# The down projection as seven block products instead of eight, in sixteen passes that add into SBUF

## The chip, the cores and the metric

One core of a Trainium2 chip runs the whole kernel as one program. The metric is the device time of one execution in microseconds. A profiled execution has, beside its time, a span: the stretch from the first to the last recorded instruction.

## What is computed

The reference is one encoder block on 512 tokens of width 2048, all in float32. The attention half is the same in both kernels. The change is in the second matrix product of the feed-forward half:

```
u = rmsnorm(x, norm_mlp_g) @ w_up            # 512 x 8192
x = x + square(relu(u)) @ w_down             # 8192 x 2048, the down projection
return rmsnorm(x, norm_final_g)
```

TensorE multiplies in a reduced format. So each float32 operand is split into a rounded high part and the rest (`wh` and `wl` of a weight, two halves of one tile for an activation), and three matmuls (high·high, high·low, low·high) stand for one. The split costs a cast on ACT and a subtraction on DVE per operand tile.

## The kernel before, in words

The stages run one after the other: attention, output projection, up projection, down projection, final norm.

The **up projection** (lines 579 to 612) makes u transposed, 32 blocks q of 256 features. Each block is a 2x2 block product with seven products instead of eight: `quad` (line 460) loads four weight blocks `b` from HBM and makes four sums of them on DVE (line 469), `parts` splits the seven weight operands (lines 94 and 95), and `prod` (line 583) runs 24 matmuls of 128x256 for each. The relu and square follow at line 611, and POOL stores 512 KB of the result to the DRAM tensor `ud` (line 612).

The **down projection** (lines 615 to 690) is a plain product. The 8192 features are cut into four chunks g of 2048. For each chunk, eight loads `ur` (line 629) bring the activations from `ud`, and each is split into `uT` (line 630). Then come four passes n over 512 output columns each. In a pass eight weight units u are loaded and split (`load_unit`, lines 72 to 91, the pools `raw`, `wh` and `wl` with three buffers each), and each serves all four token tiles t: `mm3` (lines 97 to 100) issues three matmuls of 128x512 for each of its two k tiles. After a pass four DVE instructions add the four PSUM banks, times the per-token factor `qs`, to the residual `x1` in SBUF (`add`, line 644).

There are 16 such passes of 192 matmuls, 3072 in all. The last pass (lines 659 to 690) goes token tile by token tile instead: each tile's sum of squares, `rstd_of` (line 102), four scalings and four output DMAs follow while TensorE works on the next tile. Only the fourth tile's chain is left behind the last matmul.

The code is written through a scheduler: `tc.high_priority(offset=...)` lets an instruction take an earlier place on its engine, but each engine and each queue then runs its list in the listed order. SP issues nearly all loads, POOL the stores to DRAM. The pool `rx` has six buffers of 512 KB, shared by the blocks `b` of the up projection and the `ur` tiles.

## Time and profile before

| quantity | value |
|---|---|
| median of 3 runs | 2201.66 us (2200.47 to 2202.65) |
| profiled execution, its own time | 2200.84 us |
| its span | 2199.1 us |
| TensorE busy (matmuls) | 2169.4 us, 99% of the span |
| VectorE (DVE) busy | 1241.8 us, 56% |
| ScalarE (ACT) busy | 834.8 us, 38% |
| GpSimd (POOL) busy | 211.3 us, 10% |
| DMA engines, mean rate | 125 GB/s |

The profiled execution's time is 1.74 us longer than its span; this part lies around the recorded instructions. An engine's share says how long it had something in work. It doesn't say that the end waits for it: that is read from the chain of work that ended last, and from the idle time in front of an engine's instructions. DMA-issuing instructions are not counted as busy time of their engine.

### The profile page before, as it was taken

The numbers are of one execution on the slowest core, as the hardware profiler recorded it, in microseconds if no ns is written. First come the engines' busy times: TensorE is split into PE (matmuls) and PEld (weight loads), VectorE is DVE, ScalarE is ACT, GpSimd is POOL, SyncE is SP. The second block draws the span as 40 slices with busy tenths as digits, with TensorE's granted clock in tenths as the row PEclk, the third lists the DMA queues.
The fourth block names the chain that finished last, engine by engine and source line by source line (L and its number), as shares of the span: only waits on it lengthen the run. The fifth ranks groups of instructions, "written<-read, shape, count | busy, mean of one in ns | idle before, by whom it ended". The sixth has DMA issues, their size and how long they took to land.

```text
span 2199.1 us, 31164 instructions
## 1 busy us (share of the span) xinstructions
PE 2169.4 (99%) x12988; PEld 1938.2 (88%) x12988; DVE 1241.8 (56%) x1462; ACT 834.8 (38%) x1191; POOL 211.3 (10%) x189
## 2 busy tenths in 40 slices
PE   7999999999999998999999999999999999999998
PEld 6889989888988888999999999998888888888886
DVE  6656566565574448777778777774233334234233
ACT  4444444444454434444444444442122123113232
POOL 5222122122120000000000000000000000000002
PEclk9999999999999999999999999999999999999999
DMA  6332232232243632333343334347234235223242
GB/s 214 116 110 86 92 110 88 90 110 91 78 145 135 222 110 97 125 132 128 125 145 130 127 127 144 135 147 275 98 120 156 96 100 169 96 96 115 98 142 87
DMA packets 79533, 275.26 MB, mean 125 GB/s; under 512 B 9696, under 2 KB 9888, under 8 KB 78880
## 3 DMA queue, kind: packets, MB, share of 16 engines
q1 hardware_dynamic: 69312, 240.29, 32.7%
q0 software_dynamic: 9648, 32.46, 4.5%
q8 instruction: 101, 1.65, 0.3%
q10 hardware_dynamic: 432, 0.53, 0.1%
q14 instruction: 40, 0.33, 0.0%
HBM read 240.73 MB, written 30.25 MB: 123 GB/s over the span
## 4 chain that ended last, share of the span: by engine, by line
PE 97%; DVE 1%; ACT 1%; issue 1%; DMA 0%; SPq 0%; ACTq 0%; DVEq 0%
PE pm L587 29%; PE pm L100 11%; PE pm L99 11%; PE pm L98 11%; PE pa L141 8%; PE pa L100 7%; PE pa L99 7%; PE pa L98 7%; PE pb L100 1%; PE pb L99 1%; PE pb L98 1%; PE pc L100 1%; PE pc L99 1%; PE pc L98 1%; PE pc L291 1%; PE pc L292 1%
## 5 line engine op out<-in xcount | busy, mean ns | idle before, releaser
L90 DVE TENSOR_TENSOR wl<-raw,wh 128x1024 fp32r<-128x1024 f32 (+1 forms) x219 | 269.3, 1230 | 518.3 <-ACT wh L89 517.2
L89 ACT CAST wh<-raw 128x1024 fp32r<-128x1024 f32 (+1 forms) x250 | 262.3, 1050 | 672.9 <-PE pm L100 470.6
L99 PE MATMUL pm<-wl,uT 128*128 128x512 f32 x968 | 376.6, 389 | 0.0
L100 PE MATMUL pm<-wh,uT 128*128 128x512 f32 x968 | 376.6, 389 | 0.0
L98 PE MATMUL pm<-wh,uT 128*128 128x512 f32 x968 | 376.6, 389 | 0.0
L587 PE MATMUL pm<-s,wh 128*128 128x256 f32 x1536 | 281.2, 284 | 3.8 <-ACT p L592 2.2
L587 PE MATMUL pm<-a,wh 128*128 128x256 f32 x1536 | 274.8, 282 | 0.8 <-ACT wh L94 0.8
L587 PEld LDWEIGHTS pm<-s,wh 128*128 128x128 f32 x1536 | 240.8, 193 | 4.5 <-ACT p L592 2.4
L587 PEld LDWEIGHTS pm<-a,wh 128*128 128x128 f32 x1536 | 235.5, 189 | 1.2 <-ACT wh L94 1.0
L95 DVE TENSOR_TENSOR wl<-ts,wh 128x1024 fp32r<-128x1024 f32 x128 | 154.9, 1223 | 117.5 <-ACT wh L94 117.5
L587 PE MATMUL pm<-s,wl 128*128 128x256 f32 x768 | 218.2, 284 | 0.0
L98 PEld LDWEIGHTS pm<-wh,uT 128*128 128x128 f32 x968 | 181.7, 188 | 37.8
L99 PEld LDWEIGHTS pm<-wl,uT 128*128 128x128 f32 x968 | 181.7, 188 | 37.8
L100 PEld LDWEIGHTS pm<-wh,uT 128*128 128x128 f32 x968 | 181.7, 188 | 37.7
L141 PE MATMUL pa<-wh,hT 128*128 128x256 f32 x1024 | 200.7, 290 | 13.7 <-DVE hT L166 7.3
L587 PE MATMUL pm<-a,wl 128*128 128x256 f32 x768 | 212.1, 282 | 0.0
L94 ACT CAST wh<-ts 128x1024 fp32r<-128x1024 f32 x128 | 132.7, 1052 | 196.1 <-PE pm L587 180.3
L100 PE MATMUL pa<-hT,wl 128*128 128x512 f32 x512 | 201.5, 394 | 0.0
L99 PE MATMUL pa<-hT,wh 128*128 128x512 f32 x512 | 200.9, 392 | 0.0
L98 PE MATMUL pa<-hT,wh 128*128 128x512 f32 x512 | 200.4, 391 | 0.0
L141 PEld LDWEIGHTS pa<-wh,hT 128*128 128x128 f32 x1024 | 167.9, 197 | 18.2 <-DVE hT L166 8.5
L94 ACT CAST wh<-b 128x1024 fp32r<-128x1024 f32 x96 | 101.0, 1052 | 160.4 <-PE pm L587 121.3
(240 smaller groups left out, 3432.7 us busy)
## 6 DMA issues: line engine op xcount, KB each, us to landing
b<-in_w_up SPq DMA_DIRECT2D x128, 512.0 KB, 3.7
raw<-in_w_down SPq DMA_DIRECT2D x128, 512.0 KB, 3.3
raw<-in_w_out SPq DMA_DIRECT2D x32, 512.0 KB, 3.6
ud<-c POOLq DMA_DIRECT2D x32, 512.0 KB, 3.1
ur<-ud SPq DMA_DIRECT2D x32, 512.0 KB, 4.8
raw<-in_w_dq SPq DMA_DIRECT2D x16, 512.0 KB, 3.3
raw<-in_w_dk SPq DMA_DIRECT2D x16, 512.0 KB, 3.3
raw<-in_w_nv SPq DMA_DIRECT2D x16, 512.0 KB, 3.4
```

The costliest lines, as they stand in the source:

```text
L89: nc.scalar.copy(out=wh[:, cs], in_=raw[:, cs])
L90: eng.tensor_sub(out=wl[:, cs], in0=raw[:, cs], in1=wh[:, cs].bitcast(F32))
L94: nc.scalar.copy(out=hi, in_=src)
L95: (eng or nc.vector).tensor_sub(out=lo, in0=src, in1=hi.bitcast(F32))
L98: nc.tensor.matmul(out=ps, lhsT=lh, rhs=rh, start=first, stop=False)
L99: nc.tensor.matmul(out=ps, lhsT=lh, rhs=rl, start=False, stop=False)
L100: nc.tensor.matmul(out=ps, lhsT=ll, rhs=rh, start=False, stop=last)
L141: nc.tensor.matmul(out=ps[t], lhsT=a, rhs=b[:, k, :], start=first and i == 0, stop=last and i == 2, skip_group_check=True)
L291: nc.tensor.matmul(out=ps, lhsT=xq[:, s, ts], rhs=kx[:, s, :], start=True, stop=False)
L292: nc.tensor.matmul(out=ps, lhsT=xq[:, s, ts], rhs=ky[:, s, :], start=False, stop=True)
L587: nc.tensor.matmul(out=ps, lhsT=a[:, k], rhs=b[:, k], start=first and k + i == 0, stop=last and k == 7 and i == 2, skip_group_check=True)
```

## The change

Now the down projection too is made of 2x2 block products. The features are cut into eight chunks c of 1024, the output columns into two halves n of 1024, which gives sixteen passes. The tokens are split in two halves of 256, the chunk's features in two halves of 512, and the column half into two blocks h of 512. A pass has seven products of 24 matmuls of 128x512: 168 instead of 192.

**Operands of a chunk** (`chunk_operands`): four `ur` loads in rows of 1 KB (after, line 628), four sums on DVE (lines 638, 641, 645, 647) and seven splits, in the same `rx` pool. **Weights of a pass** (`down_weights`): ten plain loads by SP (line 661), four more loads issued by POOL that add onto a block already loaded (line 663, `accum_op`), for the sums t1 = b11+b12 and t3 = b22+b12; two sums t2 and t4, two tiles each, on DVE (line 669); fourteen splits.

**Results** (`to_y`): no product is scaled; each is added to one or two of the four quarters of y in SBUF. Of the seven additions of a pass, five are DVE instructions on 128x2x512 with one operand in PSUM (line 753). The other two (first and sixth product) are an ACT copy (line 750) and a DMA by POOL that adds onto y (line 751). In chunk 0 the first write of each quarter is an ACT copy (line 747).

**The end**: x1 is no longer held in SBUF. In the last pass `finish` (lines 701 to 704) loads it in pieces, scales y by `qs` and adds it, and takes the squares; `times_g` (line 708) multiplies by the final gain; `norm_out` (lines 711 to 725) does the norm and the output DMAs of one token tile. The tiles 0 and 1 are finished first. The seventh product is cut in two blocks of 128 tokens, b = 0 and b = 1, and line 798 adds each to y.

The core of the diff:

```
+    psD = ctx.enter_context(tc.tile_pool(name="psD", bufs=4, space=bass.MemoryType.PSUM, reuse_waits="tile"))
+    wd = ctx.enter_context(tc.tile_pool(name="wd", bufs=11, reuse_waits="tile"))
+    y = ypool.tile([P, NT, DM], F32, name="y")
+    def chunk_operands(c):
+        def load(m, th):
+            t = rx.tile([P, 4, 256], F32, name="ur", tag="b")
+            nc.sync.dma_start(out=t, in_=ud[4 * c:4 * c + 4, :, (2 * m + th) * 256:(2 * m + th + 1) * 256].rearrange(
+                "j p t -> p j t"))
+            return t
+        with tc.high_priority(offset=700):
+            u11, u22, u21, u12 = load(0, 0), load(1, 1), load(0, 1), load(1, 0)
...
+            nc.vector.tensor_sub(out=f1, in0=u22, in1=u21)
+            split(o[0][:, 0], o[0][:, 1], u11)
+            split(o[1][:, 0], o[1][:, 1], f1)
+            nc.vector.tensor_add(out=f2, in0=f1, in1=u11)
...
+            nc.vector.tensor_sub(out=f2, in0=f2, in1=u12)
+            split(o[3][:, 0], o[3][:, 1], f2)
+            nc.vector.tensor_sub(out=u11, in0=u11, in1=u21)
...
+    def down_weights(c, n):
+        def load(u, i, j=None):
+            with tc.high_priority(offset=ah):
+                t = wd.tile([P, 1024], F32, name="b", tag="b")
+                nc.sync.dma_start(out=t, in_=w_down[c, n, u, i])
+                if j is not None:
+                    nc.gpsimd.dma_start(out=t, in_=w_down[c, n, u, j], accum_op=ALU.add)
+            return t
...
+        yield [parts(load(u, 0)) for u in range(2)]
+        t1 = [load(u, 0, 1) for u in range(2)]
+        yield [parts(t) for t in t1]
+        b22 = [load(u, 3) for u in range(2)]
+        t2 = [add(t1[u], b22[u]) for u in range(2)]
+        yield [parts(t) for t in t2]
...
-        for n in range(4):
-            cs = slice(n * 512, (n + 1) * 512)
-            po = [psm() for _ in range(NT)]
...
+            def to_y(ps, th, h, neg, fresh=False, dma=False):
+                ys = y[:, 2 * th:2 * th + 2, n * 1024 + h * 512:n * 1024 + h * 512 + 512]
+                if c == 0 and fresh:
+                    nc.scalar.mul(ys, ps, -1.0 if neg else 1.0)
+                elif dma:
+                    st = wd.tile([P, 2, 512], F32, name="st", tag="st", bufs=2)
+                    nc.scalar.copy(out=st, in_=ps)
+                    nc.gpsimd.dma_start(out=ys, in_=st, accum_op=ALU.add)
+                else:
+                    nc.vector.tensor_tensor(out=ys, in0=ys, in1=ps, op=ALU.subtract if neg else ALU.add)
...
+            w11, w1, w2 = next(ops), next(ops), next(ops)
+            prod(pU, o[0], w11, True)
+            to_y(pU, 0, 0, False, fresh=True, dma=not end)
+            prod(pW, o[1], w1, True)
+            to_y(pW, 1, 1, True, fresh=True)
...
+            for b in range(2):
+                prod(pU, o[6], w4, False, blocks=(b,))
+                ys = y[:, 2 + b, 1024:1536]
+                nc.vector.tensor_add(out=ys, in0=ys, in1=pU[:, b])
+                finish(2 + b, 1, 0, 1)
+                norm_out(2 + b, 2)
```

Three places where the lists of the engines change. First the border between up and down projection. The list of DVE before, from the next to last result of the last up block to the first weight units (`c` is a result of the up projection, `uT` an activation operand, `wl` a weight's low part):

```order
L605 SCALAR_TENSOR_TENSOR c<-pm,p_14512 128x256
L90 TENSOR_TENSOR wl<-raw,wh 128x1024
L95 TENSOR_TENSOR uT<-ur,uT 128x1024
L607 SCALAR_TENSOR_TENSOR c<-pm,u_14482 128x256
L95 TENSOR_TENSOR uT<-ur,uT 128x1024
L90 TENSOR_TENSOR wl<-raw,wh 128x1024
L95 TENSOR_TENSOR uT<-ur,uT 128x1024 x2
L611 SCALAR_TENSOR_TENSOR c<-c 128x1024
L90 TENSOR_TENSOR wl<-raw,wh 128x1024 x8
```

DVE now, from the same result (line 608) on. Some rows ahead of it stands the last but one result (line 606, 605 before), and right behind that the operand sum of line 647:

```order
L608 SCALAR_TENSOR_TENSOR c<-pm,u_14482 128x256
L95 TENSOR_TENSOR uT<-ur,uT 128x1024
L645 TENSOR_TENSOR uf<-uf,ur 128x1024
L95 TENSOR_TENSOR uT<-ur,uT 128x1024 x2
L612 SCALAR_TENSOR_TENSOR c<-c 128x1024
L95 TENSOR_TENSOR uT<-uf,uT 128x1024
L95 TENSOR_TENSOR wl<-b,wh 128x1024 x2
L638 TENSOR_TENSOR uf<-ur 128x1024
L641 TENSOR_TENSOR uf<-uf,ur 128x1024
L669 TENSOR_TENSOR ts<-b 128x1024
L95 TENSOR_TENSOR wl<-b,wh 128x1024
```

The two splits of the first product's weights stand at `wl<-b x2`. Behind them now come two sums for the operands of chunk 1 (lines 638 and 641), ahead of the sum and the split that the second product needs. SP's list before, at the border:

```order
L465 DMA b<-in_w_up 128x1024 x122
L629 DMA ur<-ud 128x1024 x4
L80 DMA raw<-in_w_down 128x1024
L629 DMA ur<-ud 128x1024
L80 DMA raw<-in_w_down 128x1024
L629 DMA ur<-ud 128x1024 x5
L80 DMA raw<-in_w_down 128x1024 x2
L629 DMA ur<-ud 128x1024 x2
L80 DMA raw<-in_w_down 128x1024
```

SP's list now:

```order
L465 DMA b<-in_w_up 128x1024 x122
L628 DMA ur<-ud 128x4x256 x6
L661 DMA b<-in_w_down 128x1024 x11
L628 DMA ur<-ud 128x4x256 x2
L661 DMA b<-in_w_down 128x1024 x15
```

The first six `ur` loads are the four of chunk 0 and two of chunk 1. They stand ahead of the first eleven weight loads, and the other two loads of chunk 1 behind them.

Second, the steady state on DVE. One pass before, between two passes' additions to the residual:

```order
L90 TENSOR_TENSOR wl<-raw,wh 128x1024 x8
L644 SCALAR_TENSOR_TENSOR x_0_14617<-pm,qs,x_0_14617 128x512
L644 SCALAR_TENSOR_TENSOR x_1_14618<-pm,qs,x_1_14618 128x512
L644 SCALAR_TENSOR_TENSOR x_2_14619<-pm,qs,x_2_14619 128x512
L644 SCALAR_TENSOR_TENSOR x_3_14620<-pm,qs,x_3_14620 128x512
L90 TENSOR_TENSOR wl<-raw,wh 128x1024 x8
```

Now, the second half of a pass with n = 1, in which the next chunk's operands are made:

```order
L95 TENSOR_TENSOR uT<-ur,uT 128x1024 x2
L95 TENSOR_TENSOR wl<-b,wh 128x1024
L753 TENSOR_TENSOR y<-y,pd 128x2x512
L95 TENSOR_TENSOR wl<-b,wh 128x1024
L638 TENSOR_TENSOR uf<-ur 128x1024
L95 TENSOR_TENSOR uT<-ur,uT 128x1024
L95 TENSOR_TENSOR wl<-b,wh 128x1024
L95 TENSOR_TENSOR wl<-ts,wh 128x1024
L641 TENSOR_TENSOR uf<-uf,ur 128x1024
L95 TENSOR_TENSOR wl<-ts,wh 128x1024
L669 TENSOR_TENSOR ts<-ts,b 128x1024
L753 TENSOR_TENSOR y<-y,pd 128x2x512
```

An addition (line 753) is no longer in a group at the pass's end but follows each product, with splits, sums and operands of later products between.

Third, the last pass. DVE before, the first token tile of four:

```order
L644 SCALAR_TENSOR_TENSOR x_0_14617<-pm,qs,x_0_14617 128x512
L679 TENSOR_TENSOR ssf<-v_18562,ssq 128x1
L105 TENSOR_SCALAR vf<-ssf 128x1
L107 RECIPROCAL rf<-rf 128x1
L108 TENSOR_TENSOR tf<-rf 128x1
L109 TENSOR_TENSOR tf<-tf,vf 128x1
L110 TENSOR_SCALAR tf<-tf 128x1
L111 TENSOR_TENSOR rf<-rf,tf 128x1
L684 SCALAR_TENSOR_TENSOR x_0_14617<-x_0_14617,rf,gF 128x512
L687 TENSOR_SCALAR x_0_14617<-x_0_14617,rf 128x512
```

DVE now, from behind the addition of the seventh product of the pass before and one split; the last split shown is the first one of the fourth product's weights:

```order
L702 SCALAR_TENSOR_TENSOR y<-y,qs,xr 128x1024 x4
L669 TENSOR_TENSOR ts<-ts,b 128x1024
L95 TENSOR_TENSOR wl<-b,wh 128x1024
L753 TENSOR_TENSOR y<-y,pd 128x2x512
L708 TENSOR_TENSOR y<-y,gF 128x1024
L95 TENSOR_TENSOR wl<-ts,wh 128x1024
L708 TENSOR_TENSOR y<-y,gF 128x1024
L95 TENSOR_TENSOR wl<-ts,wh 128x1024
L708 TENSOR_TENSOR y<-y,gF 128x1024 x2
L753 TENSOR_TENSOR y<-y,pd 128x2x512
L669 TENSOR_TENSOR ts<-ts,b 128x1024
L95 TENSOR_TENSOR wl<-b,wh 128x1024 x2
```

The eight instructions of lines 702 and 708 for the column half n = 0 now stand between the splits of the second, third and fourth product.

## Rows read from the trace of the kernel before

**Rows 1.** The page, busy time of the engines (us, share of the span, instructions).
```profile
PE 2169.4 (99%) x12988; PEld 1938.2 (88%) x12988; DVE 1241.8 (56%) x1462; ACT 834.8 (38%) x1191; POOL 211.3 (10%) x189
```

**Rows 2.** The page, the chain that ended last, shares by engine.
```profile
PE 97%; DVE 1%; ACT 1%; issue 1%; DMA 0%; SPq 0%; ACTq 0%; DVEq 0%
```

**Rows 3.** Busy time by stretch (us of each engine, instructions, clock, DMA share, GB/s).
```profile
1492.50:2145.00 652.50, 652.50 (x2880) 540.28 (x2879) 223.96 (x211) 161.46 (x168) 0.53 (x1) 1.00 0.37 126
2150.00:2190.00 40.00, 39.89 (x172) 31.87 (x170) 10.61 (x31) 6.81 (x15) 10.51 (x7) 1.00 0.21 79
```

**Rows 4.** Timeline of PE at both ends of the down projection (start, us).
```profile
1492.10 0.28 PE L587 MATMUL pm<-a,wl 128*128 128x256 f32 x1
1492.22 0.40 PE L98 MATMUL pm<-wh,uT 128*128 128x512 f32 x1
...
2189.51 0.39 PE L100 MATMUL pm<-wh,uT 128*128 128x512 f32 x1
```

**Rows 5.** Groups by form, 1492.5 to 2145 (xcount | busy, mean ns | idle before).
```profile
L90 DVE TENSOR_TENSOR wl<-raw,wh 128x1024 fp32r<-128x1024 f32 x120 | 147.0, 1225 | 401.4 <-ACT wh L89 401.4
L89 ACT CAST wh<-raw 128x1024 fp32r<-128x1024 f32 x119 | 125.7, 1057 | 472.3 <-PE pm L100 470.6 <-DMA raw<-in_w_down 1.5
L644 DVE SCALAR_TENSOR_TENSOR x<-pm,qs,x 128x512 f32<-128x512 f32 x57 | 41.4, 748 | 14.8 <-PE pm L100 14.8
```

**Rows 6.** Groups by form of the whole span, same columns.
```profile
L587 PE MATMUL pm<-s,wh 128*128 128x256 f32 x1536 | 281.2, 284 | 3.8 <-ACT p L592 2.2 <-DVE s L453 1.1 <-ACT u L592 0.6
L469 DVE TENSOR_TENSOR ts<-ts,b 128x1024 f32<-128x1024 f32 x64 | 78.2, 1222 | 0.8
...
L527 DVE TENSOR_TENSOR xb<-xb,pa 128x512 f32<-128x512 f32 x8 | 5.4, 684 | 1.3 <-DMA xb<-in_x 1.3
```

**Rows 7.** Busy time of a stretch in which transfers pile up.
```profile
1490.00:1500.00 10.00, 10.00 (x56) 8.63 (x55) 8.16 (x9) 4.89 (x6) 0.53 (x1) 1.00 1.03 408
```

**Rows 8.** DMA issues of the page (KB each, us to landing).
```profile
raw<-in_w_down SPq DMA_DIRECT2D x128, 512.0 KB, 3.3
...
ud<-c POOLq DMA_DIRECT2D x32, 512.0 KB, 3.1
ur<-ud SPq DMA_DIRECT2D x32, 512.0 KB, 4.8
```

**Rows 9.** Timeline of DVE at the border (start, us).
```profile
1486.76 0.42 DVE L605 SCALAR_TENSOR_TENSOR c<-pm,p 128x256 f32<-128x256 f32 x1 [0.50 <-PE pm L587]
...
1488.79 1.22 DVE L95 TENSOR_TENSOR uT<-ur,uT 128x1024 fp32r<-128x1024 f32 x1
1489.93 0.42 DVE L607 SCALAR_TENSOR_TENSOR c<-pm,u 128x256 f32<-128x256 f32 x1
1490.26 1.22 DVE L95 TENSOR_TENSOR uT<-ur,uT 128x1024 fp32r<-128x1024 f32 x1
1491.40 1.22 DVE L90 TENSOR_TENSOR wl<-raw,wh 128x1024 fp32r<-128x1024 f32 x1
```

**Rows 10.** Busy time by stretch, first products of the up projection.
```profile
845.00:852.00 7.00, 2.51 (x15) 1.82 (x14) 7.00 (x4) 6.46 (x6) 0.00 (x0) 0.88 0.00 1
852.00:856.00 4.00, 3.84 (x18) 3.84 (x19) 4.00 (x5) 1.21 (x1) 0.00 (x0) 0.50 0.00 0
856.00:860.00 4.00, 4.00 (x31) 4.00 (x31) 4.00 (x3) 2.17 (x3) 0.00 (x0) 0.86 0.00 0
```

**Rows 11.** Timeline of the end (start, us).
```profile
2189.93 0.75 DVE L644 SCALAR_TENSOR_TENSOR x<-pm,qs,x 128x512 f32<-128x512 f32 x1 [6.76 <-PE pm L100]
...
2191.53 0.16 DVE L679 TENSOR_TENSOR ssf<-v,ssq 128x1 f32<-128x1 f32 x1 [0.85 <-ACT junk L648]
...
2193.24 1.34 ACT L689 ACTIVATE x<-x,rf 128x512 f32<-128x512 f32 x2 [1.06 <-DVE rf L111]
2193.85 0.48 DVE L687 TENSOR_SCALAR x<-x,rf 128x512 f32<-128x512 f32 x1
```

More of the change, by code (lines that the diff above doesn't have):

```diff
@@ L549, in hymba_kernel @@
     ps_es.close()
-    psM = ctx.enter_context(tc.tile_pool(name="psM", bufs=8, space=bass.MemoryType.PSUM, reuse_waits="tile"))
+    ps_up = ctx.enter_context(ExitStack())
+    psM = ps_up.enter_context(tc.tile_pool(name="psM", bufs=8, space=bass.MemoryType.PSUM, reuse_waits="tile"))
     def psm():
@@ L615, in hymba_kernel @@
     up_es.close()
+    ps_up.close()
+    psD = ctx.enter_context(tc.tile_pool(name="psD", bufs=4, space=bass.MemoryType.PSUM, reuse_waits="tile"))
     ypool = ctx.enter_context(tc.tile_pool(name="ypool", bufs=1, reuse_waits="tile"))
[L617 to L690 removed]
@@ new lines, in down_weights, with add, parts @@
+    def down_weights(c, n):
+        ah = 3000
+        def load(u, i, j=None):
[5 more added lines that the diff above has]
+            return t
+        def add(a, b):
+            with tc.high_priority(offset=ah):
+                t = wpool.tile([P, 1024], F32, name="ts", tag="raw")
+                nc.vector.tensor_add(out=t, in0=a, in1=b)
+            return t
+        def parts(t):
+            with tc.high_priority(offset=ah):
+                h = wpool.tile([P, 1024], F32R, name="wh", tag="wh")
+                l = wpool.tile([P, 1024], F32R, name="wl", tag="wl")
+                split(h, l, t)
+            return h.rearrange("p (k c) -> p k c", k=2), l.rearrange("p (k c) -> p k c", k=2)
+        yield [parts(load(u, 0)) for u in range(2)]
[4 more added lines that the diff above has]
+        yield [parts(t) for t in t2]
+        yield [parts(t) for t in b22]
+        t3 = [load(u, 3, 1) for u in range(2)]
+        yield [parts(t) for t in t3]
+        b21 = [load(u, 2) for u in range(2)]
+        t4 = [add(t2[u], b21[u]) for u in range(2)]
+        yield [parts(t) for t in b21]
+        yield [parts(t) for t in t4]
@@ new lines, in hymba_kernel, with finish @@
+    ss3 = keep.tile([P, NT, 3], F32, name="ss3")
+    gF = []
+    def finish(t, n, h, col):
+        lo, w = (n * 1024, 1024) if h is None else (n * 1024 + h * 512, 512)
+        ys = y[:, t, lo:lo + w]
+        xr = wd.tile([P, 1024], F32, name="xr", tag="b")
+        nc.sync.dma_start(out=xr[:, :w], in_=x1d[t][:, lo:lo + w])
+        nc.vector.scalar_tensor_tensor(out=ys, in0=ys, scalar=qs[:, t:t + 1], in1=xr[:, :w], op0=ALU.mult, op1=ALU.add)
+        junk = wd.tile([P, 1024], F32, name="junk", tag="junk", bufs=1)
+        nc.scalar.activation(out=junk[:, :w], in_=ys, func=AF.Square, accum_out=ss3[:, t, col:col + 1])
@@ new lines, in times_g, with norm_out @@
+    def times_g(t, lo, w):
+        g = gF[lo // 1024][:, lo % 1024:lo % 1024 + w]
+        nc.vector.tensor_mul(out=y[:, t, lo:lo + w], in0=y[:, t, lo:lo + w], in1=g)
+    def norm_out(t, late):
+        ss = keep.tile([P, 1], F32, name="ssf", tag="ssf")
+        nc.vector.tensor_reduce(out=ss, in_=ss3[:, t], axis=AX.X, op=ALU.add)
+        r = rstd_of(keep, ss, DM, 1, "f")
+        for i in (late, 0, 5 - late, 1):
+            qq = slice(i * 512, (i + 1) * 512)
+            z = y[:, t, qq]
+            if i == late:
+                nc.vector.scalar_tensor_tensor(out=z, in0=z, scalar=r, in1=gF[1][:, (i - 2) * 512:(i - 1) * 512],
+                                               op0=ALU.mult, op1=ALU.mult)
+            elif i >= 2:
+                nc.vector.tensor_scalar_mul(z, z, r)
+            else:
+                nc.scalar.mul(z, z, r)
+            nc.sync.dma_start(out=out[t * P:(t + 1) * P, qq], in_=z)
@@ L738 @@
     wu = a("w_up", 2, 8, P, 32, 2, P).transpose(3, 0, 4, 2, 1, 5).reshape(32, 4, P, 1024)
-    wd = units(a("w_down", DFF, DM), 512)
+    wd = a("w_down", 8, 2, 2, 2, P, 2, 2, 512).transpose(0, 5, 1, 3, 6, 4, 2, 7).reshape(8, 2, 2, 4, P, 1024)
     arrays = {
@@ L755 @@
         "in_w_up": wu,
-        "in_w_down": wd.reshape(4, 4, 8, P, 1024).transpose(1, 0, 2, 3, 4),
+        "in_w_down": wd,
         "in_norm_final_g": a("norm_final_g", 1, DM),
```

123 lines of the change are left out of this document (59 added, 64 removed).

## Prediction

> **What bounds the kernel now.** I read the page first. TensorE is busy 99% of the span, DVE 56%, ACT 38% [rows 1], and the chain that ended last is TensorE for 97% [rows 2]. A busy share is an average, so next I looked at the down projection alone. From 1492.50 to 2145.00 the windows show 652.50 us of matmul in 652.50 us, at full clock, while DVE works 224 us, ACT 161 us and the DMA engines have a share of 0.37 [rows 3]. So this stage is TensorE and nothing else: 2880 matmuls in 652.5 us make 0.2266 us each. The last pass is a little slower, 172 in 40 us or 0.2326 [rows 3]. The stage runs from 1492.22 to 2189.51 plus the last matmul's 0.39, thus 697.7 us [rows 4]. Nobody else is near a limit: DVE's weight splits wait 401 us for ACT, and ACT's casts wait 471 us for TensorE to free a buffer [rows 5]. There is room for work on the other engines; whether the new work fits is the question.
>
> **TensorE's work.** 3072 matmuls become 16 x 168 = 2688 of the same shape. At 0.2266 that is 609.1 us in place of 697.7: **-88.6 us**. Were all of them as slow as the last pass now, 2688 x 0.2326 = 625.2, a gain of only 72.5; I take the steady row, as 15 of 16 passes show it. A product of 24 matmuls is then 5.44 us, a pass 38.1 us, and two passes, or a chunk, 76.2 us.
>
> **DVE.** A 128x1024 subtraction is busy 1.22 us [rows 5, 6], but queued ones start 1.14 apart (1490.26, 1491.40) [rows 9]. Per chunk I count 28 weight splits, 8 weight sums, 7 operand splits, 4 operand sums and 10 additions to y: 57 instructions, 65 us at 1.14 out of 76.2. The additions read PSUM; the nearest row is 128x512 in 684 ns [rows 6], so 1024 elements cost up to 1.37. ACT has 28 + 7 casts and 4 copies of 1.06 us, 41 of 76.2. Before, DVE had 224 us of work in 652; now it has 85% of TensorE's time. A pass with n = 1 holds 33 of the 57, 37.6 us of 38.1: no slack on the average, and only the splits made ahead (three buffers each of `wh` and `wl`) carry it. The nearest row for what such a pattern costs is the up projection, also seven products with sums and splits: in its largest group the matmuls of line 587 waited 3.8 us in 32 blocks [rows 6]. I take **+5 us** for the whole steady state, with 0 and 20 as its ends.
>
> **DMA.** When transfers pile up the engines move 408 GB/s at a share of 1.03 [rows 7], so 512 KB take 1.28 us; a lone load lands after 3.3 us [rows 8], so about 2.0 are fixed. A pass has 10 plain weight loads and on average 2 `ur` loads: 15.4 us of 38.1. It also has 6 adding transfers of 512 KB, for which the trace of before has no row. Their floor is a plain transfer, 1.28 us. I take two transfers, 2.6 us, since what stands at the destination has to be fetched too; 15.4 + 15.6 = 31 us of 38.1 then, and it hides. The other end is a rival below. The Trainium skill speaks against this part: "Collectives: The Full Stack", section "The bandwidth ceiling: the fold count and why AG ≠ RS ≠ AR", says that an add in the DMA path needs two source reads, two descriptors per chunk instead of one, and that this halved the measured rate of a reduce against a copy. By that page the sum stays as it is, as the price equals the one taken; no run here shows it yet.
>
> **The start of the stage** is no longer covered. In before the first down matmul follows the last up matmul after 0.12 us [rows 4]. Now SP issues six `ur` loads first; the sixth, for chunk 1, takes the `rx` buffer that line 647 last reads. That sum stands right behind the up result of old line 605, which starts at 1486.76 [rows 9]; 0.42 + 1.22 later it is 1488.4, 3.8 us before the last up matmul is through. Behind it on SP wait all eleven first weight loads and then chunk 1's third `ur` load, on which line 638 waits. Line 638 in turn stands in DVE's list ahead of the second product's sum and splits. From -3.8 on, 13 transfers x 1.28 = 16.6 give 12.8, the fixed 2.0 give 14.8, one adding transfer among them 17.4. Then lines 638, 641, 669 and the split, 4 x 1.14 = 4.6, give 22.0. The second product should have begun at 5.4, so 16.6 us are lost. Its second half waits for three more DVE steps, 3.4 us against a half product of 2.7: +0.7. After such an idle time the clock is low: in the first up products TensorE was busy 2.51 of 7 us, and the granted clock was then 0.50 for 4 us and 0.86 for 4 more [rows 10], which loses 2.0 + 0.5. In all **+19.8**. The lower end, if the load lands early and only DVE's backlog counts (nine long instructions and a short one behind line 647, 10.6 us, then the 4.6: second product at 11.4), is 6.0 + 0.7 = 6.7; the upper, if all four adding loads of the pass come in between, is 19.8 + 7.8 = 27.6.
>
> **The last pass.** Eight instructions of lines 702 and 708 now stand among the splits. From the addition of the pass before to the first split of the fourth product DVE has 18 instructions, 20.5 us; TensorE gets there after 3 x 5.44 = 16.3. That is 4.2 lost. The block b = 1 of the seventh product waits for line 798 of block 0, which reads the same PSUM tile: one 128x512 addition with its wait, 0.8. **+5.0**, ends 0 and 8.
>
> **The tail.** In before, from the last matmul's end at 2189.9 to the span's end at 2199.1 there are 9.2 us, one chain of addition, square, norm and scalings [rows 11]. Now DVE's list has the norms of three more token tiles behind or around the last addition. One, from line 679 to the end of 687, takes 2191.53 to 2194.33, 2.8 us [rows 11]. Three in a row: **+8.4**, ends 0 and 11.
>
> **Sum.** -88.6 + 5.0 + 19.8 + 5.0 + 8.4 = -50.4. Against the profiled execution's own 2200.84 us that is 2150.4. The median of the three runs lies 0.8 above the profiled one, so I forecast **2151 us**, 2140 to 2166 if the mechanism is right.
>
> **Rivals.**
> *The adding transfers bind (slower).* Nothing in the profile prices them. With a us each a pass needs 15.4 + 6a of the DMA engines. Above a = 3.8 this is longer than TensorE's 38.1; the gain of 50.4 is gone when a pass is 3.15 us longer, at 41.2, so at a = 4.3, some 3.4 times a plain transfer. At a = 5 a pass is 45.4 and the time 2151 + 16 x 7.3 = 2268. For it: a reduction by DMA has more to do per byte, and POOL issues them in order behind a plain load. Against: 2.6 has much room to 4.3. The skill's section named above, which finds the adding rate half of a copy's, leaves it below that point. Chance 0.12.
> *DVE is the bound in the second halves.* If DVE, with every instruction waiting on ACT or PSUM, needs 1.22 for 28 and 1.37 for the five additions, a pass with n = 1 takes 41.0 against 38.1: 8 x 2.9 = 23 more. For it: 37.6 of 38.1 already at the best pace. Against: the n = 0 passes have 24 instructions and can make splits ahead. 2151 - 5 + 23 = 2169, up to 2190 with TensorE at the slower rate of the last pass. Chance 0.19.
> *Start and last pass hide.* If chunk 1's load lands before DVE gets to line 638 and the splits of the last pass are made ahead, the start costs 6.7 and the last pass 0.8: -88.6 + 5.0 + 6.7 + 0.8 + 8.4 = -67.7, thus 2134. For it: before shows no idle TensorE here at all. Against: SP's list puts the blocked load ahead of the weights. Chance 0.15.
>
> **Chances.** Forecast 0.52, adding transfers 0.12, DVE 0.19, hidden start 0.15, and 0.02 for an outcome near no change, with the adding transfers close to 4.3. A difference of 0.2%, 4.4 us, is about what can be told from none. Faster: 0.52 + 0.19 + 0.15 = 0.86; same 0.02; slower 0.12. The range 2128 to 2190 takes in the hidden start with its steady term near 0, and the DVE rival with the slower rate; the adding transfers are left outside.
>
> **What would show it.** Right: windows of the down stage with TensorE 100% busy and some 168 matmuls in 38.1 us; one hole of 10 us or more between the first and the second product, with DVE's line 638 waiting for `ur`; a short hole ahead of the fourth product of the last pass; a tail of 17 us; adding transfers that land in a few us. Wrong: regular holes in every pass. If they end on POOL's transfers it is the first rival, if on DVE's splits the second. The sum fails too if a matmul is slower than 0.2266, or if the additions to y keep a PSUM tile so long that TensorE waits for it.

## The result, and the profile after

The changed kernel takes 2174.34 us (median of 4 runs, 2170.92 to 2177.16) against 2201.19 (4 runs, 2200.47 to 2202.65): a ratio of 0.9876 with a 95% interval of 0.9859 to 0.9894. It is 1.2% faster, clear of the noise, and 2174 lies in the stated range of 2128 to 2190. But it lies outside the 2140 to 2166 that were named for the forecast mechanism: the gain is 26.9 us where 50 were forecast. The parts do not cancel either: TensorE's work and the tail came out as forecast, and start, middle and last pass each lost more. The page after, with the lines that answer to [rows 1, 2, 8]:

```profile
PE 2094.5 (96%) x12604; PEld 1867.4 (86%) x12604; DVE 1544.0 (71%) x1710; ACT 988.1 (45%) x1339; POOL 285.1 (13%) x273
...
PE 84%; DMA 6%; DVE 6%; ACT 2%; issue 1%; SPq 0%; ACTq 0%; DVEq 0%; POOLq 0%
...
b<-in_w_down SPq DMA_DIRECT2D x160, 512.0 KB, 5.3
...
b<-in_w_down POOLq DMA_DIRECT2D x64, 512.0 KB, 8.4
...
ur<-ud SPq DMA_DIRECT2D x32, 512.0 KB, 5.3
y<-st POOLq DMA_DIRECT2D x28, 512.0 KB, 8.1
```

TensorE lost its 384 matmuls, and the chain that ended last is TensorE for only 84%, where it was 97%: DMA and DVE have 6% each. The two POOL rows are the adding transfers, of weights and of results. They take over 8 us to land; a plain weight load takes 5.3, where it took 3.3.

From the start times of the matmuls on PE's timeline I took each pass from its first matmul to the first of the next; the end of the up projection is the start of its last matmul plus 0.12 us, the step to the next matmul in before. The seven passes with n = 0 behind the first last 38.08 us (38.17 in one), which is the 168 x 0.2266 of the prediction. Set against these 38.08 us, every loss has a place:

| term | forecast | measured |
|---|---|---|
| matmuls, 697.7 to 16 x 38.08 = 609.3 | -88.6 | -88.4 |
| start: gap behind the up projection 4.5, first pass 65.2 in place of 38.1 | +19.8 | +31.6 |
| middle: the seven passes n = 1 (n = 0: 0.1) | +5.0 | +13.1 |
| last pass, 48.7 | +5.0 | +10.6 |
| tail, from 9.2 to 17.0 | +8.4 | +7.8 |
| last up matmul earlier | 0 | -0.8 |
| sum of the span, 2199.1 to 2173.0 | -50.4 | -26.1 |

**Start.** PE's timeline, the matmuls in front of which it stood idle (in brackets: idle time and what ended it):

```profile
1495.88 0.79 PE L741 MATMUL pd<-wh,uT 128*128 128x512 f32 x1 [4.35 <-ACT wh L94]
1497.34 0.80 PE L741 MATMUL pd<-wl,uT 128*128 128x512 f32 x1 [0.66 <-DVE wl L95]
1508.82 0.80 PE L741 MATMUL pd<-wh,uT 128*128 128x512 f32 x1 [4.22 <-ACT wh L94]
1525.66 0.79 PE L741 MATMUL pd<-wl,uT 128*128 128x512 f32 x1 [16.05 <-DVE wl L95]
```

DVE's timeline in the same stretch:

```profile
1496.07 2.35 DVE L95 TENSOR_TENSOR wl<-b,wh 128x1024 fp32r<-128x1024 f32 x2
1520.85 1.23 DVE L638 TENSOR_TENSOR uf<-ur 128x1024 f32<-128x1024 f32 x1 [22.43 <-issue]
...
1523.25 1.22 DVE L669 TENSOR_TENSOR ts<-b 128x1024 f32<-128x1024 f32 x1
1524.39 1.22 DVE L95 TENSOR_TENSOR wl<-b,wh 128x1024 fp32r<-128x1024 f32 x1
```

The mechanism is the forecast one: line 638 stands ahead of the second product's sum and split, and waits 22.4 us for a load of chunk 1. The profile names only "issue" as what ended that wait; the loads themselves show it, SP's issues and the time to landing of the `ur` loads in this stretch:

```profile
1498.52 1.75 SPq L628 DMA_DIRECT2D ur<-ud  x2
```

```profile
DMA to landing us min/median/max: 3.4/13.8/22.4
```

The first of the two was issued at 1498.5 and landed some 22.3 us later, so it was there at 1520.8, just ahead of line 638. It was to be there 17.4 us after the last up matmul (1491.4); the sum began after 29.5. POOL's issues tell the first reason: the last two of line 663's four in this stretch, and the time to landing of the four:

```profile
1506.45 0.85 POOL L663 DMA_DIRECT2D b<-in_w_down  x1 [6.51 <-DMA b<-in_w_down]
1510.23 0.84 POOL L663 DMA_DIRECT2D b<-in_w_down  x1 [2.93 <-DMA b<-in_w_down]
```

```profile
DMA to landing us min/median/max: 8.9/9.4/12.4
```

The last one landed 8.9 us after 1510.23, at 1519.1. So all four adding loads of the pass went ahead of the load that line 638 waits for, where the forecast counted one; a store of 512 KB to `ud` (issued at 1495.90) went ahead too. The windows tell the second reason (the last three columns are the granted clock, the DMA share and GB/s):

```profile
1490.00:1495.00 5.00, 1.53 (x14) 1.33 (x12) 5.00 (x6) 1.87 (x4) 0.00 (x0) 0.93 1.01 386
...
1500.00:1505.00 5.00, 4.60 (x18) 3.39 (x16) 0.00 (x0) 0.36 (x1) 0.00 (x0) 0.89 1.03 345
1505.00:1510.00 5.00, 0.80 (x1) 0.29 (x1) 0.00 (x0) 1.70 (x2) 0.85 (x1) 0.79 1.06 275
1510.00:1515.00 5.00, 0.00 (x0) 0.00 (x0) 0.00 (x0) 1.04 (x1) 0.84 (x1) 0.50 1.04 279
```

The DMA engines are full, and yet the rate falls from 386 to 275 GB/s, where I had counted 408 throughout [rows 7].

**Middle.** All n = 0 passes are whole; each n = 1 pass has one to three short holes ahead of a low-part matmul, at the fourth and fifth product. The chain of waits of one such pass (start, us, what):

```profile
1714.89 1.24 DVE wl L95
...
1716.15 5.04 DMA b<-in_w_down
...
1721.98 8.04 DMA b<-in_w_down
...
1730.10 1.23 DVE ts L669
1731.33 1.13 DVE y L753
1732.46 1.14 DVE wl L95
```

Read it from the top: a split frees a buffer, a plain load fills it in 5.0 us, the adding load behind it takes 8.0, line 669 has waited for that, and behind it in DVE's list stand the addition to y and the split that TensorE needs.

**Last pass.** DVE's timeline shows a wait that the prediction doesn't have: line 702 waits for the transfer that adds onto y.

```profile
2109.76 1.28 DVE L702 SCALAR_TENSOR_TENSOR y<-y,qs,xr 128x1024 f32<-128x1024 f32 x1
2115.71 3.68 DVE L702 SCALAR_TENSOR_TENSOR y<-y,qs,xr 128x1024 f32<-128x1024 f32 x3 [4.67 <-DMA y<-st]
```

On PE the largest hole stands in the middle of the second product, not ahead of the fourth as forecast (there it is 0.99):

```profile
2121.71 0.79 PE L741 MATMUL pd<-wl,uT 128*128 128x512 f32 x1 [5.88 <-DVE wl L95]
```

The wait of block b = 1 for line 798 is 0.78 us, for which 0.8 was forecast.

**Tail.** ACT's scalings of the four token tiles, one norm after the other, all behind the last matmul's end at 2155.98, and SP's output transfers:

```profile
2159.16 1.32 ACT L724 ACTIVATE y<-y,rf 128x512 f32<-128x512 f32 x2
...
2166.84 1.34 ACT L724 ACTIVATE y<-y,rf 128x512 f32<-128x512 f32 x2 [1.00 <-DVE rf L111]
...
2159.42 10.24 SPq L725 DMA_DIRECT2D out_y<-y  x16
```

All sixteen output transfers, 256 KB each, are issued behind the last matmul. In before, only the four of the fourth token tile were.

### The profile page after: what moved, and what is told of

The parts are those of the page before. It is cut to its first block, busy times and chain, and to the rows that moved or that the text cites. A ratio compares the mean times of both kernels' runs of the same rounds, so it can differ in the third digit from the quotient of the medians.

```text
span 2173.0 us, 31223 instructions
## 1 busy us (share of the span) xinstructions
PE 2094.5 (96%) x12604; PEld 1867.4 (86%) x12604; DVE 1544.0 (71%) x1710; ACT 988.1 (45%) x1339; POOL 285.1 (13%) x273
## 3 DMA queue, kind: packets, MB, share of 16 engines
q0 software_dynamic: 26480, 80.70, 17.1%
## 4 chain that ended last, share of the span: by engine, by line
PE 84%; DMA 6%; DVE 6%; ACT 2%; issue 1%; SPq 0%; ACTq 0%; DVEq 0%; POOLq 0%
PE pm L588 29%; PE pd L741 19%; PE pa L141 8%; PE pa L99 7%; PE pa L98 7%; PE pa L100 7%; DMA b<-in_w_down 6%; DVE wl L95 2%; PE pb L100 1%; PE pb L98 1%; PE pb L99 1%; PE pc L99 1%; PE pc L100 1%; PE pc L98 1%; DVE y L753 1%
## 5 line engine op out<-in xcount | busy, mean ns | idle before, releaser
L741 PE MATMUL pd<-wh,uT 128*128 128x512 f32 x1792 | 558.2, 393 | 9.3 <-ACT wh L94 8.6
L94 ACT CAST wh<-b 128x1024 fp32r<-128x1024 f32 x256 | 268.6, 1049 | 386.2 <-PE pd L741 215.0
L741 PEld LDWEIGHTS pd<-wh,uT 128*128 128x128 f32 x1792 | 339.8, 190 | 81.3 <-ACT wh L94 9.2
L741 PE MATMUL pd<-wl,uT 128*128 128x512 f32 x896 | 354.2, 395 | 31.0 <-DVE wl L95 30.8
L95 DVE TENSOR_TENSOR wl<-b,wh 128x1024 fp32r<-128x1024 f32 x256 | 311.2, 1219 | 62.9 <-ACT wh L94 60.8
L95 DVE TENSOR_TENSOR wl<-ts,wh 128x1024 fp32r<-128x1024 f32 x192 | 232.7, 1221 | 131.0 <-ACT wh L94 130.7
L741 PEld LDWEIGHTS pd<-wl,uT 128*128 128x128 f32 x896 | 169.8, 190 | 75.4 <-DVE wl L95 40.6
L89 ACT CAST wh<-raw 128x1024 fp32r<-128x1024 f32 (+1 forms) x129 | 134.5, 1043 | 200.2 <-PE pa L99 72.1
L90 DVE TENSOR_TENSOR wl<-raw,wh 128x1024 fp32r<-128x1024 f32 (+1 forms) x98 | 120.9, 1235 | 117.0 <-ACT wh L89 115.6
L141 PE MATMUL pa<-wl,hT 128*128 128x256 f32 x512 | 147.6, 289 | 0.0
```

The costliest lines, as they stand in the source:

```text
L89: nc.scalar.copy(out=wh[:, cs], in_=raw[:, cs])
L90: eng.tensor_sub(out=wl[:, cs], in0=raw[:, cs], in1=wh[:, cs].bitcast(F32))
L94: nc.scalar.copy(out=hi, in_=src)
L95: (eng or nc.vector).tensor_sub(out=lo, in0=src, in1=hi.bitcast(F32))
L141: nc.tensor.matmul(out=ps[t], lhsT=a, rhs=b[:, k, :], start=first and i == 0, stop=last and i == 2, skip_group_check=True)
L741: nc.tensor.matmul(out=ps[:, b], lhsT=l, rhs=r[:, k], start=first and u + k + i == 0, stop=last and u == 1 and k == 1 and i == 2, skip_gro ...
```

## The experiments

Twelve kernels, all edits of the changed one. The last up matmul ends between 1489.4 and 1492.6 from run to run, so a single time is good to a few us; the losses of the stretches, taken as above, say more. They have a spread too: in kernels whose edit leaves them alone the start loses 29.7 to 31.6, n = 1 8.5 to 13.0 and the last pass 9.1 to 10.6. "n = 1" is the sum of the seven such passes, "n = 0" that of the six in the middle, "14" the pass ahead of the last.

| kernel | time | start | n = 1 | n = 0 | 14 | last | tail |
|---|---|---|---|---|---|---|---|
| changed | 2174.3 | 31.6 | 13.0 | 0.0 | 0.1 | 10.6 | 17.0 |
| e1 plain sums | 2155.5 | 25.6 | 1.1 | 0.0 | 1.6 | 9.1 | 17.0 |
| e2 start order | 2161.8 | 21.9 | 10.5 | 0.0 | 0.3 | 9.9 | 17.1 |
| e3 last y by DVE | 2164.5 | 29.8 | 10.1 | 0.1 | 0.1 | 5.5 | 16.8 |
| e4 y by DVE | 2174.4 | 29.8 | 15.4 | 2.4 | 4.8 | 4.0 | 17.0 |
| e5 one more buffer | 2162.1 | 31.3 | 1.0 | 0.0 | 4.6 | 7.1 | 16.8 |
| e6 t2 for t4 | 2198.4 | 29.7 | 18.9 | 17.2 | 6.0 | 5.9 | 17.0 |
| e7 both ends | 2141.7 | 7.7 | 8.5 | 0.3 | 0.1 | 8.2 | 13.7 |
| e8 sums on POOL | 2182.9 | 7.5 | 38.5 | 11.1 | 1.6 | 9.4 | 13.5 |
| e9 own norm tiles | 2167.4 | 30.1 | 10.7 | 0.1 | 0.1 | 9.1 | 16.8 |
| e10 e7 and e5 | 2133.0 | 10.0 | 0.6 | 0.0 | 0.6 | 6.6 | 14.1 |
| e11 e10 and e9 | 2132.0 | 10.0 | 0.3 | 0.0 | 0.9 | 6.6 | 13.0 |
| e12 two output queues | 2131.9 | 9.7 | 0.4 | 0.0 | 0.4 | 6.6 | 13.7 |

**e1, plain transfers for the weight sums.**

```
-                    nc.gpsimd.dma_start(out=t, in_=w_down[c, n, u, j], accum_op=ALU.add)
+                    nc.gpsimd.dma_start(out=t, in_=w_down[c, n, u, j])
```

> Leaves out the addition in the four weight transfers of a pass (t1 and t3): they are plain transfers of the same size, in the same place of the same queue, so the sums are no sums. The order of all engines is that of the changed kernel, where the first pass with its start lost 31.7 us against 38.1, the seven second-half passes n = 1 lost 13.0 together and the DMA share of a steady pass was 0.93. Theory A (an adding transfer is dear, and that is what the start and the n = 1 passes wait for): share of a steady pass near 0.70, the n = 1 passes lose under 5 together, the start under 26; time about 2158 to 2164. Theory B (DVE's list is too full in n = 1, DMA is bystander): the n = 1 passes still lose 11 or more, time within 4 of 2174.

Theory A held: with the same lists on every engine the n = 1 passes lose 1.1 in place of 13.0, and the start 25.6. The time lies 3 below what it expected, and the share is 0.80, not 0.70. The windows over four passes (4 to 7), of the changed kernel and of e1:

```profile
1678.26:1835.10 156.84, 154.24 (x673) 125.66 (x672) 132.24 (x115) 79.24 (x78) 23.72 (x25) 1.00 0.93 241
```

```profile
1668.30:1821.05 152.75, 152.74 (x673) 125.97 (x672) 132.05 (x115) 79.29 (x78) 18.62 (x25) 1.00 0.80 248
...
1500.00:1510.00 10.00, 3.86 (x15) 2.46 (x13) 0.00 (x0) 3.11 (x3) 1.06 (x2) 0.82 1.03 417
```

This prices the adding transfer. The DMA engines work 0.93 x 156.84 / 4 = 36.5 us per pass and in e1 0.80 x 152.75 / 4 = 30.6; the difference, over four transfers, is 1.5 us each. With 16 plain and 2 adding ones in e1, and all adding ones taken as equal, a plain transfer is 1.5 and an adding one 3.0. The last row is e1's start: 417 GB/s at full engines, where the changed kernel moved 275 to 345.

**e2, chunk 1's operand work behind the first pass.** The marks are the first pass's last weight split on DVE and its last weight load on SP.

```
-        o = chunk_operands(c)
+        if c == 1:
+            with tc.issue_after(mark["dve"]), tc.issue_after(mark["sp"]):
+                o = chunk_operands(c)
+        else:
+            o = chunk_operands(c)
...
```

> Only chunk 1's operand work is moved: its four loads behind the last weight load of the first pass in SP's list, its DVE work behind the last weight split of the first pass. Theory S1 (the hole between first and second product comes from line 638 standing ahead of the second product's split and waiting for a load that stands behind eleven others): the hole of 4.2 + 16.1 us falls under 7, the start with the first pass loses 12 to 18 in place of 31.7, time about 2157 to 2162. Theory S2 (the weights and their adding transfers themselves arrive that late, the order only hides it): the start still loses over 25, time 2168 or more.

Between the two theories: the hole of 4.2 + 16.1 at the second product is down to 3.05 + 0.58, yet the start still loses 21.9. PE's timeline (line 752 there is line 741 of the changed kernel) shows the next thing that is late, the fourth product's second half:

```profile
1507.35 0.73 PE L752 MATMUL pd<-wh,uT 128*128 128x512 f32 x1 [3.05 <-ACT wh L680]
...
1529.98 0.79 PE L752 MATMUL pd<-wl,uT 128*128 128x512 f32 x1 [4.83 <-DVE wl L681]
```

The order explains some 10 us. The rest goes with weights that come late: the holes, and the slower matmuls behind them (0.73 to 0.80 us in these rows, where the steady ones show 0.39). Behind the last hole the granted clock was 0.50, the lower of its two levels, from 1529.90 to 1534.00.

**e3, no adding transfer to y in the pass ahead of the last.**

```
-                elif dma:
+                elif dma and not (c == 7 and n == 0):
```

> Only in the pass ahead of the last are the two adding transfers to y replaced by additions on DVE, so that line 702 of the last pass waits for no transfer. Theory L1 (the largest hole of the last pass, 6.3 us and more at half clock, comes from line 702 waiting 11 us for the transfer that adds to y): the last pass loses 4 to 6 in place of 10.6, time about 2168 to 2170. Theory L2 (the eight instructions of lines 702 and 708 in DVE's list alone make it): it still loses 9 or more, and the pass ahead, with two DVE additions more, about 2 more; time 2174 to 2177.

L1 held: the last pass loses 5.5, half of 10.6, and the pass ahead 0.1 as before. DVE's waits in the last two passes of the changed kernel had this row, and e3 has none on `y<-st`:

```profile
DVE y L702 <- DMA y<-st: 4.7, 1, 4.7
```

The time fell by 10; 5 of it is this pass, the rest lies in stretches that the edit doesn't touch (middle 2.9, start 1.8), which is what single runs differ by.

**e4, all additions to y on DVE.**

```
-                elif dma:
+                elif False:
```

> All additions to y on DVE, no adding transfer to y at all: DVE has 35 instructions in a pass n = 1 (39.9 us at 1.14 against 38.1 of matmul), the DMA engines two adding transfers fewer. Theory A (adding transfers are what the passes wait for): the n = 1 passes lose under 9 together in place of 13.0, and the last pass 4 to 6 in place of 10.6; time 2163 to 2168. Theory B (DVE's list is the bound in n = 1): the n = 1 passes lose 20 or more together, and n = 0 passes begin to lose too; time 2176 or more.

Neither. The n = 1 passes lose 15.4, between the two theories, and the n = 0 passes begin to lose (2.4 and 4.8): two more DVE instructions cost about what two fewer adding transfers give. In each four passes DVE now has 123 instructions where it had 115. The DMA share prices the additions to y as well:

```profile
1674.16:1832.21 158.05, 154.96 (x673) 125.37 (x672) 140.74 (x123) 72.01 (x70) 14.01 (x16) 1.00 0.77 213
```

0.77 x 158.05 / 4 is 30.4 us per pass against 36.5, so one of these two costs 3.0 too.

**e5, twelve buffers for loaded weights in place of eleven.**

```
-    wd = ctx.enter_context(tc.tile_pool(name="wd", bufs=11, reuse_waits="tile"))
+    wd = ctx.enter_context(tc.tile_pool(name="wd", bufs=12, reuse_waits="tile"))
```

> Only the pool of loaded weights has 12 buffers in place of 11; the lists of the engines in the middle passes stay as they are. In the changed kernel the seven middle passes n = 1 lost 13.0 us together, in e1 with plain transfers 1.1. Theory A1 (it is the landing: a plain load and an adding one behind it start when a buffer comes free and land too late for line 669): with a buffer more they start earlier and the n = 1 passes lose under 7. Theory A2 (it is the DMA engines' throughput, 0.93 busy): loads start earlier but land no earlier, the passes lose 11 to 14. Time 2166 to 2169 by A1, 2172 to 2176 by A2; start, last pass and tail as before in both.

A1, and clearly: 13.0 becomes 1.0 (and the time is 4 below what A1 expected, 2166). The window over passes 4 to 7, and DVE's waits in the middle (total, times, longest), first of e5, then the same row of the changed kernel:

```profile
1673.83:1826.41 152.58, 152.58 (x674) 126.09 (x672) 132.31 (x115) 79.20 (x78) 23.56 (x25) 1.00 0.92 249
...
DVE ts L669 <- DMA b<-in_w_down: 5.6, 6, 1.1
```

```profile
DVE ts L669 <- DMA b<-in_w_down: 16.7, 6, 3.1
```

The DMA share stays at 0.92 and DVE does the same 132 us of work in 152.6. So neither was the bound: the transfers were issued too late, for want of a free buffer. The pass ahead of the last and the last lose 11.7 together as in the changed kernel (10.7): that was left as it was.

**e6, t2 for t4 in the seventh product.**

```
-        yield [parts(t) for t in t4]
+        yield [parts(t) for t in t2]
```

> Leaves out the sum t4 of every pass (the seventh product multiplies by t2 instead): two DVE instructions fewer in a pass, 31 in a pass n = 1, all transfers as before. Theory AB (the n = 1 passes lose where a late adding transfer meets a DVE list without slack, so either cure helps): they lose under 6 together in place of 13.0. Theory A alone (the transfer is late whatever DVE does): 10 or more. Time 2163 to 2168 by AB, 2171 or more by A.

A miss of the edit. The additions for t4 are still made and only not used, so DVE has not an instruction fewer, and the test says nothing on DVE's load. What it did change is that t2 keeps its `ts` buffer, one of three, until the seventh product. The middle passes lose 36.1 in place of 13.0, and line 669's waits for loads grow from 16.7 to 52.2 us. That the held buffer does it is argued here, not shown.

**e7, both ends.** As e2 and e3; the first pass's t1 and t3 by plain loads and DVE; b21 ahead of t3 in the last pass (loads, splits and products). Of the diff, the part on the first pass's sums:

```
-                if j is not None:
+                if j is not None and not (c + n == 0):
                     nc.gpsimd.dma_start(out=t, in_=w_down[c, n, u, j], accum_op=ALU.add)
+                elif j is not None:
+                    t2 = wd.tile([P, 1024], F32, name="b", tag="b")
+                    nc.sync.dma_start(out=t2, in_=w_down[c, n, u, j])
+                    (nc.vector).tensor_add(out=t, in0=t, in1=t2)
```

> Three edits at the ends, none in the middle: chunk 1's operand work behind the first pass as in e2, the sums t1 and t3 of the first pass alone on DVE with plain loads, and at the end the additions to y on DVE in the pass ahead of the last as in e3 and b21 loaded and split ahead of t3 in the last pass, so that the norms of token tiles 0 and 1 can start a product earlier. If the adding transfers are what is left of the start's loss, it falls from 21.9 in e2 to 12 to 17; the rival (loads as such, plain or adding, come too late, because no buffer is free before the up projection ends) keeps it over 20. Last pass 4 to 6, tail 12 to 15 in place of 17.0. Middle passes lose 10 to 13. Time 2144 to 2153; by the rival 2154 or more.

Better than expected: the start loses 7.7, the time is 2141.7. PE's timeline of the start has only two holes left (line 761 there is line 741 of the changed kernel):

```profile
1494.34 0.49 PE L761 MATMUL pd<-wh,uT 128*128 128x512 f32 x1 [2.35 <-ACT wh L684]
1497.79 0.79 PE L761 MATMUL pd<-wl,uT 128*128 128x512 f32 x1 [2.95 <-DVE wl L685]
```

The start's 31.6 thus has two causes, each of which hides the other: the order alone gives 9.7 (e2), the adding transfers alone 6.0 (e1), both 23.9. The last pass, 8.2, is worse than e3's 5.5: PE now also waits 1.57 us ahead of the seventh product and 1.20 in place of 0.78 between its two blocks.

**e8, the weight sums on POOL in all passes but the first.** As e7, with no adding weight transfer.

```
-                if j is not None and not (c + n == 0):
+                if j is not None and not (True):
...
-                    (nc.vector).tensor_add(out=t, in0=t, in1=t2)
+                    (nc.vector if c + n == 0 else nc.gpsimd).tensor_add(out=t, in0=t, in1=t2)
```

> As e7, and in all other passes too the sums t1 and t3 without adding transfers: plain loads and an addition on POOL, which has little else to do. Theory A (adding transfers cost the n = 1 passes their time): DMA share of a steady pass near 0.8, the n = 1 passes lose under 3 together as in e1, time 8 to 12 below e7. Rival (additions of 2.4 to 2.7 us on POOL, as its 128x1024 subtractions took in the kernel before, come too late or slow DVE down): they lose 13 or more, time at or above e7.

The rival: 41 us slower than e7, though the DMA share fell to 0.73. The windows over four passes, a single split on DVE's timeline, and the groups by form in the middle of the stage (lines 671, 685, 677, 773 are POOL's sum, the weight split, the sum of line 669, the addition of line 753):

```profile
1664.43:1831.50 167.07, 157.94 (x674) 126.25 (x672) 156.47 (x115) 79.14 (x78) 63.17 (x24) 0.99 0.73 227
```

```profile
1697.05 3.28 DVE L685 TENSOR_TENSOR wl<-ts,wh 128x1024 fp32r<-128x1024 f32 x1
```

```profile
L671 POOL TENSOR_TENSOR b<-b 128x1024 f32<-128x1024 f32 x46 | 159.4, 3472 | 221.2 <-DMA b<-in_w_down 198.3 <-DVE y L773 12.4 <-DVE wl L685 10.4
L685 DVE TENSOR_TENSOR wl<-b,wh 128x1024 fp32r<-128x1024 f32 x114 | 147.9, 1314 | 6.5 <-ACT wh L684 6.5
L685 DVE TENSOR_TENSOR wl<-ts,wh 128x1024 fp32r<-128x1024 f32 x44 | 71.6, 1628 | 9.0 <-ACT wh L684 9.0
L773 DVE TENSOR_TENSOR y<-y,pd 128x1024 f32<-128x1024 f32 x58 | 70.2, 1210 | 0.3 <-PE pd L761 0.3
L677 DVE TENSOR_TENSOR ts<-b 128x1024 f32<-128x1024 f32 x23 | 43.9, 1907 | 8.4 <-DMA b<-in_w_down 7.8
```

POOL's addition takes 3.47 us, and DVE's instructions on two SBUF operands grow from 1.22 to 1.31, 1.63 and 1.91 on the mean, while those with an operand in PSUM stay at 1.21. The same 115 DVE instructions now fill 156.5 of 167.1 us, where the changed kernel's took 132.2 of 156.8: DVE's own time accounts for the larger part of the loss. From 1600 to 2070 line 669's sums also wait 10.5 us for loads. That may be a want of buffers, since each of the four added blocks now takes one of the eleven for itself; no run separates the two.

**e9, separate small norm tiles for each token tile.**

```
-        ss = keep.tile([P, 1], F32, name="ssf", tag="ssf")
+        ss = keep.tile([P, 1], F32, name="ssf", tag=f"ssf{t}")
...
-        r = rstd_of(keep, ss, DM, 1, "f")
+        r = rstd_of(keep, ss, DM, 1, f"f{t}")
```

> Only the small tiles of the final norm (its sum, variance, root and correction) are separate for each of the four token tiles, so that one norm need not wait for the scalings of the one before. Theory N1 (the tail of 17.0 us, 9.2 in the kernel before, is four norms kept apart by these shared tiles): it falls to 10 to 13. Theory N2 (the squares and the scalings on ACT and DVE themselves fill it): it stays at 15 or more. Time 4 to 7 below 2174 by N1, within 2 by N2.

N1 fell, for a reason that neither theory had. ACT's last scaling now ends 9.0 us behind the last matmul (2148.78), before 12.2; but the tail is 16.8, and SP's sixteen output transfers are spread over 10 us as before:

```profile
2156.40 1.33 ACT L724 ACTIVATE y<-y,rf 128x512 f32<-128x512 f32 x2 [0.31 <-DVE rf L111]
...
2152.29 9.97 SPq L725 DMA_DIRECT2D out_y<-y  x16
```

What spreads them is not the issuing itself, as the window shows:

```profile
2153.50:2164.00 10.50, 0.00 (x0) 0.00 (x0) 3.80 (x16) 3.64 (x7) 0.00 (x0) 0.50 1.03 382
```

The DMA engines are full. Sixteen transfers of 256 KB are 4.2 MB, which at 382 GB/s take 11.0 us; the first is issued 3.5 us behind the last matmul, and the first to land took 2.2.

The time is 7 lower all the same, in stretches that the edit doesn't touch (middle, start, last pass and border, about 2 each): again the spread of single runs.

**e10, e7 with the twelfth buffer.** The edits of e7 and e5.

> The edits of e7 and the twelfth buffer of e5 together. If start, middle and end are separate losses, the middle n = 1 passes lose under 2 together as in e5 and the start 6 to 10 as in e7: time 2141.7 - 9 = 2133, 2129 to 2137. If the buffer only moved the load on the DMA engines (in e5 the pass ahead of the last lost 4.6), that pass and the last lose 12 or more together and the time stays at 2137 or more.

The losses are separate: 2133.0, the middle passes lose 0.6, the start 10.0.

**e11, e10 with separate norm tiles.**

> e10 with the separate norm tiles of e9: the tail 13.7 in e7 falls to 10 or less. By N1 3 to 5 us below e10, 2126 to 2132, which would be the fastest kernel of this study; by N2 the same as e10 within 1.5.

Median 2132.01 of 5 runs (2130.42 to 2134.12), ratio to the kernel before 0.9684 (0.9670 to 0.9697). Faster than both kernels. The tail is 13.0, where N1 expected 10 or less, and the step from e10 is 1.0, as by N2; a single run of e10 can't carry so small a step, so what this piece is worth stays open.

**e12, half of the outputs issued by POOL.**

```
-            nc.sync.dma_start(out=out[t * P:(t + 1) * P, qq], in_=z)
+            (nc.sync if i >= 2 else nc.gpsimd).dma_start(out=out[t * P:(t + 1) * P, qq], in_=z)
```

> e11 with the sixteen output transfers issued half by SP and half by POOL, in place of all by SP. In e9 the norm's last scaling came 9.0 us behind the last matmul in place of 12.2 in the changed kernel, and yet the tail stayed at 16.8, since SP issued the outputs one after the other over 10 us. Theory N3 (SP's issuing is what the tail waits for once the norms are apart): the tail falls from 13.0 in e11 to 10 to 11.5, time 1.5 to 3 below e11's 2132.0. Rival (the last token tile's own chain sets the end): the tail stays at 12.5 to 13.5 and the time within 1 of e11.

The time is the rival's: 2131.88 (5 runs, 2130.87 to 2134.14), the same as e11. In e11 the last scaling ends 6.7 us behind the last matmul, and 6.4 follow; in e12 6.7 and 7.0. A shorter queue on SP gave nothing: POOL's outputs take 4.5 us to land, where SP's took 3.0 in e11. But the rival's reason, the last token tile's own chain, isn't what the trace shows. The first 10 us behind the last matmul, in e12:

```profile
2117.41:2127.41 10.00, 0.00 (x0) 0.00 (x0) 5.73 (x20) 4.55 (x10) 3.89 (x8) 0.70 1.01 365
```

The DMA engines are as full as in e9, from one queue or two. What is left of the tail is 4.2 MB of output, which starts 1.2 us ahead of the last matmul's end. Earlier outputs should then shorten it; no run tests that.

## Why the prediction was right or wrong

**TensorE's work** was right to 0.2 us: the rate of the steady passes, not that of the slower last one, carried over.

**The range.** The forecast was 2151, or 2140 to 2166 if its mechanism is right; 2174 is outside of that. It lies where the rival *DVE is the bound* was put, 2169 to 2190, and it was for that rival that the stated range reached so far up. (That rival's upper end is added up too high: 2169 and the 16 us of the slower rate are 2185.) By the time alone one would have picked that rival, and the experiments refute it. So the range held by its width; three of the five terms were too small.

**The steady state** is the step that failed most in kind. The prediction put the adding transfer at 2.6 us (measured 3.0) and a plain one at 1.28 (1.5, mixed with others), so 31 us of 38.1 were 36.5: sizes a little low, the conclusion that throughput hides still true, as e5 shows with a share of 0.92 and a loss of 1.0. What was missing is the time to land. A plain load and an adding one behind it take 5 + 8 us from the moment a buffer is free, and line 669 waits for it and keeps the splits behind it in the list waiting. "+5 with 0 and 20 as ends", taken from the up projection, held 13.1 only by its width: that stage has no transfers in series. The prediction did say that DVE has no slack on the average in n = 1, 37.6 us of 38.1. By time it has some: in one such pass of e5 (1711.91 to 1750.25) DVE is busy for 33.8 of 38.3 us, as some of the 33 listed instructions run outside of it (30 are counted). The question left out is when the buffer of each adding load comes free. Where the prediction set the price, the Trainium skill's sentence that an add needs two source reads and halves the rate ("Collectives: The Full Stack", section "The bandwidth ceiling: the fold count and why AG ≠ RS ≠ AR") agrees with e1: 3.0 against 1.5 us. The runs here show the ratio, not its reason, and that section speaks of collectives.

**The start** had the right mechanism, with SP's order, line 638 and the low clock, and one term mis-sized: 13 transfers at 1.28 us and one adding one gave a load at 17.4 us; measured 29.5. Four adding ones and a store went ahead, as the prediction's upper end had it for the four. At the prices of e1 the 14 plain and 4 adding transfers take 14 x 1.5 + 4 x 3.0 = 33 us; SP issued the sixth `ur` load at 1487.9, and 33 us later is 1520.9, where line 638 began. The rate of [rows 7] belongs to plain transfers. With four adding ones among them, full engines move 275 to 345 GB/s; in e1 417. The upper end for the whole start, 27.6, was too low as well (31.6): it had the lower prices.

**The last pass**: the 4.2 for eight instructions among the splits and 0.8 for line 798 are together about what e3 leaves, 5.5. The place was wrong, though: in e3 the hole (2.20 us, and slower matmuls behind it) stands in the second product, not ahead of the fourth. The other 5 is a wait that wasn't in the list: line 702 reads the y that a transfer of the pass before still adds to.

**The tail** was right in size, 7.8 for 8.4, and right that the norms stand one after the other. But that is not all that holds the end: the prediction put nothing for the sixteen outputs that now come behind the last matmul, and e9 shows that with the norms apart these outputs keep the tail at 16.8: 3.5 us until the first is issued, and 11.0 us of full DMA engines. So the tail's size was met in part by luck.

**Rivals.** The adding transfers did not bind as priced: 3.0 is under 3.8, and under the 3.35 that plain transfers of 1.5 would leave; in the steady passes they cost through latency instead. DVE as the bound is refuted in its plain form: no n = 0 pass loses, and with one more buffer the same list runs in 38.1 to 38.4. Its 1.37 us for an addition to y was too high as well: with an operand in PSUM 1024 elements took 1.21. The hidden start did not come, and needs both edits of e7.

## What to carry to other kernels

Ask of a transfer not only whether the engines have room, but when its buffer comes free and how long it takes to land; two transfers in series onto one buffer need a buffer more, and here that one buffer took 12 us off the n = 1 passes (e5), and 8 on top of e7 (e10). A rate taken from plain loads must not be used for a stretch that holds adding ones. And where an in-order engine is 87% busy, any wait in its list is paid by everyone behind it, so put what waits for a far transfer behind what is ready. At the end, count the bytes that are released behind the last matmul, and not only the chain of instructions.
